# Three key units of a recurrent layer share each input tile, ahead of the low-rank projections

## The chip, the cores and the metric

The kernel runs on one core of one Trainium2 chip. The metric is the device time of one execution in microseconds (us), taken as the median of several runs.

## What is computed

One inference step of a two-layer decoder: layer A is a recurrent (delta-rule) layer, layer B an attention layer. Tokens stand in columns: 512 prompt columns and 32 sample columns, 544 in all; features are 1024 = 8 tiles of 128 partitions. Only the start of layer A matters here:

```
xn = rms_norm(x, ln_g)
prev = xn shifted by one token
mixed[i] = xn + mu[i] * (prev - xn)          # i = r, k, v, z, w, a
k = mixed[k] @ w_in[k]                       # 1024 x 1024: the key projection
w_low, a_low = tanh(mixed[w] @ w_la), mixed[a] @ a_la     # 64 columns each
kk = (k * k_k), divided per head by its norm
```

Everything that follows in layer A (decays, chunk products, state, group norm, gate, output projection) needs the keys and their norms, and layer B needs layer A.

## The kernel before

Work of the start, in the order of the program:

- The eight tiles of x are loaded and squared, and their sums give one factor per token. `norm` writes a tile of xn, `mix` (L302 to L311) makes a mixed tile: ScalarE scales xn (L305 for 512 columns, L306 for 32), VectorE adds the shifted part (L307, L309). `split` (L163) makes the exact pair of the mixed tile: the rounded part by ScalarE (L166) and the remainder by VectorE or GpSimd (L167), by the letters of `ENG["xk"] = "gvgvgggv"` (g is GpSimd, v is VectorE). These eight pairs are `xk`, kept until the last key unit.
- A unit is 128 output features: `load_w` (L126) brings 512 KB of weights into one of two `wst` buffers, ScalarE rounds them (L133, `whi`) and GpSimd subtracts (L134, `wlo`); each of `whi` and `wlo` has two buffers. `dense` (L143) then does three products per input tile, whi by x rounded, whi by x remainder, wlo by x rounded, for two column halves of 256 and 288: 48 matmuls a unit. A half has one PSUM bank of the two of pool `pd`. In some units (`BOTH`, among the key units 0, 4, 5, 6, 7) the two halves advance together over the input tiles, in the others one after the other.
- `kproj` (L351) is one key unit. Behind each half come a copy of the bank to SBUF on VectorE (L104), a square on ScalarE (L357) and a matmul with `sel` (L358) that adds the squares per head into `ssp`.
- `hidden` (H in the plan) does one input tile's part of the two low-rank projections: two mixes into the two buffers of pool `mp`, and matmuls into `hps`, both banks of pool `pu` (L378).

`PLAN` is a list of such steps by hand: H0 K0 K1 H1 ... is the order in which the program is written, with a number behind the letter. It is not quite the order on the engines. The context is opened with `schedule_with_timeline_sim=True`, and a scheduler with a timeline of its own picks, for each engine, among the steps that it takes to be ready; the plan's order is their priority. Each engine then runs its list in order.

PSUM has eight banks: two each in `pd` (projections), `pt` (`ssp` in this stage), `pu` (`hps` in this stage) and `pc` (unused in this stage). Pool `bp` (tag B, ten buffers of 128 x 1088) first serves the chunk operands of a later stage.

Of the kernel before, what the change touches and what calls it, by code (L numbers as in the profile page):

```python
# [6 lines left out]
F32 = mybir.dt.float32  # L7
F32R = mybir.dt.float32r
# [6 lines left out]
P = 128  # L15
D = 1024
KT = 8
# [41 lines left out]
NR = 2  # L59
PLAN = """H0 K0 K1 H1 H2 H3 H4 H5 K2 H6 H7 K3 K4 K5 K6 K7 X3 r0 r7 N a0 r1 a1 b0 e0 b1 e1 T0  # L60
X2 r2 r3 a3 r4 a2 r6 r5 X0 v1 v3 v0 b3 e3 M0 P0 F0 F1 F2 v2 C0 C1 b2 o1 F3 C2 C3 M1
# [17 lines left out]
class Kern:  # L79
# [45 lines left out]

    def load_w(self, src, gain=None):  # L126
        nc = self.nc
        st = self.wst.tile([P, KT, P], F32, name="wst", tag="wst")
        nc.sync.dma_start(out=st, in_=src)
        hi = self.whl.tile([P, KT, P], F32R, name="whi", tag="whi")  # L130
        lo = self.whl.tile([P, KT, P], F32R, name="wlo", tag="wlo")
        if gain is None:
            nc.scalar.copy(hi, st)  # L133
            nc.gpsimd.tensor_tensor(lo, st, hi.bitcast(F32), op=ALU.subtract)  # L134
        else:
            for kt in range(KT):
                g = self.prm[:, gain, kt:kt + 1]
                nc.scalar.mul(hi[:, kt], st[:, kt], g)  # L138
                nc.vector.scalar_tensor_tensor(lo[:, kt], st[:, kt], g, hi[:, kt].bitcast(F32),  # L139
                                               op0=ALU.mult, op1=ALU.subtract)  # L140
        return hi, lo

    def dense(self, w, xs, evac, both=False):  # L143
        """three exact-part passes; both: the two column halves advance together over the inner tiles"""
        nc = self.nc
# [8 lines left out]
        for hfs in (((0, 1),) if both else ((0,), (1,))):  # L154
# [4 lines left out]
            for hf in hfs:  # L159
                c0, n = HALF[hf]  # L160
                evac(hf, c0, n, ps[hf][:, :n])

    def split(self, src, name, eng=None):  # L163
        nc = self.nc
        hi, lo = self.xpair(name)
        nc.scalar.copy(hi, src)  # L166
        (eng or nc.vector).tensor_tensor(lo, src, hi.bitcast(F32), op=ALU.subtract)  # L167
        return hi, lo

    def sq_add(self, tot, x, kt, tmp, halves=False):  # L170
        """squares of the features, summed over the tiles"""
        for c0, n in HALF if halves else ((0, NT),):
# [7 lines left out]
    def rms(self, sq, psum, sp):  # L180
        """1 / rms per token in every partition (PSUM); sq: squares summed over the tiles"""
        nc = self.nc
# [16 lines left out]

# [1 line left out]
    def layer_a(self):  # L201
        tc, nc, I, O, prm = self.tc, self.nc, self.I, self.O, self.prm
        with ExitStack() as ctx:
# [49 lines left out]

# [1 line left out]
            xt = []  # L255
# [27 lines left out]

# [1 line left out]
            sq8 = H_("sq8")  # L285
# [39 lines left out]
            def inv_rows(d):  # L325
                """reciprocal of rows in DRAM, spread over the partitions"""
                n = d.shape[0] * d.shape[1] // P
# [13 lines left out]

# [1 line left out]
            xk = []  # L343
            for kt in range(KT):
                norm(kt)
# [4 lines left out]

            def kproj(p):  # L351
                t = H_("kT")

                def evac(hf, c0, n, ps):
# [4 lines left out]
                                     start=(p == 0), stop=(p == 7))  # L359
                self.dense(self.load_w(W[p]), xk, evac, both=p in BOTH)  # L360
                if p < NR:
                    kT[p] = t
                else:
                    nc.sync.dma_start(out=scr["k"][p], in_=t)

            hps, la = [], []

            def hidden(kt):
                """one input tile's part of the low-rank hidden layers"""
                if kt == 0:  # L370
# [22 lines left out]

# [1 line left out]
            AL, RH, BK, AK = ([None] * 8 for _ in range(4))  # L395
# [41 lines left out]
            def pre_b(p):  # L437
# [7 lines left out]
                nc.vector.scalar_tensor_tensor(nb, ta, 1.0, kn, op0=ALU.add, op1=ALU.mult)  # L445
                # sample columns: alpha, rho, beta, kappa
                sq = sp.tile([P, 4, NS], F32, name="sq", tag="sq")
# [14 lines left out]
                self.eng("bk", p).tensor_tensor(bk[:, :, 64:128], c64(kp), ipv[:, :, 1:65], op=ALU.mult)  # L462
                # bonus sums
                nc.vector.scalar_tensor_tensor(kp, rT[p], pv(P_RK, p), kp, op0=ALU.mult, op1=ALU.mult)
# [4 lines left out]
            def pre_e(p):  # L469
                """bonus sums; the sample columns' products with the state"""  # L470
                kp, sq, st = POST[p]
# [4 lines left out]
                nc.sync.dma_start(out=scr["b"][p], in_=kp)  # L476
                # sample: token-major copies, products with the state
                ps = T8("sps")
# [50 lines left out]
            def tinv(g):  # L529
                """blocks of T = (1 - A)^-1 on the diagonal, for the chunks of two pairs: substitution,  # L530
                one lane per block and parity of the column; kept transposed"""
                a = tp.tile([P, 1024], F32, name="tA", tag="T", bufs=1)
# [21 lines left out]
            def tmerge(p):  # L554
                """the block below the diagonal: T21^T = T11^T (A21^T T22^T)"""
                g = p // 2
# [38 lines left out]
            def prechain(p):  # L595
                ak, bk, rh, t = AK[p], BK[p], RH[p], TT[p]
                w = ak.rearrange("p c h x -> p (c h x)")
                # stacked [T alpha; T A_kappa]
                WW[p] = w.rearrange("p (e c h x) -> p e c h x", e=2, c=4, h=2)
# [15 lines left out]
            def feed(p, i):  # L615
                """operands of two chunks: stacked [A_beta; A_kappa], keys against the end of the chunk, values"""
                bk, rh = BK[p], RH[p]
# [28 lines left out]
            def step(p, c2):  # L646
                """state in, [M0; V] or [V; M0] by head; its updates U, stacked [U; V]; state out; outputs"""
                uv = sp.tile([P, 2, 2, 64], F32, name="uv", tag="uv", bufs=2)
# [35 lines left out]
            def bonus(p):  # L684
                """bonus term and the norm's bias, kept in DRAM until the norm"""
                t = zp.tile([P, NT], F32, name="bsum", tag="Z")
# [54 lines left out]
            def gn_sample():  # L741
                """group norm, bonus of the sample columns of all pairs"""
                for p in range(8):
# [22 lines left out]
            def gn(g):  # L766
                """group norm of the prompt columns of two pairs: deviations, their reciprocals"""
                ssg, sqs = U8("ssg"), []
# [17 lines left out]
            def gn_apply(g):  # L786
                """norm, bonus"""
                normed.add(g)
# [8 lines left out]
            def zproj(p):  # L797
                """gate; applied at once where the norm comes first"""
                hold = p // 2 not in normed
# [44 lines left out]
            def xzsplit():  # L844
                for kt in range(KT):
# [3 lines left out]
            xv, xz = [], []  # L849
            fns = dict(K=kproj, H=hidden, N=lambda p: key_norms(), r=rproj, a=pre_a, b=pre_b, e=pre_e, T=tinv, v=vproj,  # L850
                       M=tmerge, P=prechain, F=lambda j: feed(j // 4, j % 4), C=lambda j: step(j // 4, j % 4), o=bonus,
# [5 lines left out]

# [1 line left out]
            gx = [self.split(Y[p], "g") for p in range(8)]  # L859
# [25 lines left out]

# [1 line left out]
    def layer_b(self):  # L887
        tc, nc, I, O, prm = self.tc, self.nc, self.I, self.O, self.prm
        with ExitStack() as ctx:
# [29 lines left out]

            # normalised input  # L920
            def load_h(kt):
# [70 lines left out]
            def scores(st, l):  # L992
                """scores and exponentials of the window (l = 0) or of the strided groups (l = 1)"""
                Q, K = st["Q"], st["K"]
# [32 lines left out]
            def join(st, p):  # L1027
                """factors that put both row orders on a common maximum and sum"""
                stats = [st["stats", l] for l in range(2)]
# [28 lines left out]
            def attend(st, i):  # L1058
                """weights transposed, times the values: window (own block, block before), two strided groups"""
                l, half, g = ((0, 1, 0), (0, 0, 0), (1, 0, 1), (1, 1, 2))[i]  # L1060
# [170 lines left out]

            # output projection, residual, final norm
            gx = [self.split(G[p], "g") for p in range(8)]
# [37 lines left out]
    def new_state(self):  # L1271
        """The recurrent state of the sample group after its tokens, on GpSimd."""
        tc, nc, I, O = self.tc, self.nc, self.I, self.O
# [38 lines left out]
def prep(inp):  # L1312
# [27 lines left out]
    c0, c1, c2 = (f[f"cache_kv_g{g}"].reshape(8, -1, 2, 4, 4, 64) for g in range(3))  # L1340
    # keys: [quad, b half, head pair, chunk, (head, c), b, 256 rows]; values: [quad, b half, chunk, 128 rows, b, (head, c)]
    rows = np.arange(128)
# [111 lines left out]
```

## Time and profile before

| what | us |
|---|---|
| median of 3 runs | 1532.63 |
| lowest, highest run | 1529.68, 1542.64 |
| span of the profiled execution | 1545.5 |
| TensorE busy in it | 1429.4 (92%) |

The profiled execution is one of its own; its span, from the first to the last instruction, is the only time that the profile gives for it. A line of the timeline has start, duration, engine, line of the kernel, operation, what is written from what, the shape, the count of instructions merged, and in brackets the idle time before it and what ended that. Matmuls overlap in time, so their step is read from their starts. The granted clock of a window is the profile's; what level TensorE had is read from the pace of the matmuls as well.

### The profile page before, as it was taken

The numbers are of one execution on the slowest core, as the hardware profiler recorded it, in microseconds if no ns is written. First come the engines' busy times: TensorE is split into PE (matmuls) and PEld (weight loads), VectorE is DVE, ScalarE is ACT, GpSimd is POOL, SyncE is SP. The second block draws the span as 40 slices with busy tenths as digits, with TensorE's granted clock in tenths as the row PEclk, the third lists the DMA queues.
The fourth block names the chain that finished last, engine by engine and source line by source line (L and its number), as shares of the span: only waits on it lengthen the run. The fifth ranks groups of instructions, "written<-read, shape, count | busy, mean of one in ns | idle before, by whom it ended". The sixth has DMA issues, their size and how long they took to land.

```text
span 1545.5 us, 32046 instructions
## 1 busy us (share of the span) xinstructions
PE 1429.4 (92%) x12144; PEld 1184.9 (77%) x12144; DVE 999.4 (65%) x2612; ACT 656.0 (42%) x1808; POOL 531.3 (34%) x763
## 2 busy tenths in 40 slices
PE   2998978998988989999989999999999999999996
PEld 2676966676767757998877788977889788897776
DVE  7429494748577356789995787745468455684635
ACT  5447452343433355344633335444345443554322
POOL 6125355434545122896776772000000000000111
PEclk9999978776869698999999999999999999999998
DMA  4123635233323024564345653445534366344543
GB/s 141 49 84 127 197 98 144 69 81 91 91 79 88 19 59 120 162 193 146 117 136 164 202 190 116 141 134 193 190 113 138 127 202 198 105 143 131 192 136 105
DMA packets 140586, 201.24 MB, mean 130 GB/s; under 512 B 76864, under 2 KB 80640, under 8 KB 140432
## 3 DMA queue, kind: packets, MB, share of 16 engines
q1 hardware_dynamic: 121456, 137.48, 29.7%
q10 hardware_dynamic: 16416, 54.41, 11.1%
q0 software_dynamic: 2560, 7.31, 1.4%
q8 instruction: 95, 1.56, 0.4%
q14 instruction: 59, 0.48, 0.1%
HBM read 150.90 MB, written 34.87 MB: 120 GB/s over the span
## 4 chain that ended last, share of the span: by engine, by line
PE 67%; DVE 17%; DMA 8%; ACT 3%; issue 2%; SPq 2%; POOL 0%; DVEq 0%; ACTq 0%; POOLq 0%
PE dps L152 39%; DVE wlo L139 3%; PE ops L1078 3%; PE sps L1015 2%; PE ptp L1070 2%; DVE tX L548 2%; PE sps L1011 2%; PE spo L1161 2%; PE sc L1117 1%; PE ops L1082 1%; DVE tT L546 1%; PE cps L675 1%; DMA ot<-exp 1%; PE cps L678 1%; PE hps L378 1%
## 5 line engine op out<-in xcount | busy, mean ns | idle before, releaser
L152 PE MATMUL dps<-hn,whi 128*128 128x256 f32 (+1 forms) x2560 | 512.0, 295 | 5.9 <-DVE ho L873 2.4
L152 PEld LDWEIGHTS dps<-hn,whi 128*128 128x128 f32 x2560 | 406.5, 190 | 30.3 <-issue 18.9
L152 PE MATMUL dps<-hn,wlo 128*128 128x288 f32 (+1 forms) x1280 | 377.5, 295 | 4.5 <-DVE wlo L139 4.3
L138 ACT ACTIVATE whi<-wst,prm 128x128 fp32r<-128x128 f32 x640 | 201.3, 391 | 224.5 <-PE dps L152 175.4
L139 DVE SCALAR_TENSOR_TENSOR wlo<-wst,prm,whi 128x128 fp32r<-128x128 f32 x640 | 251.9, 447 | 36.6 <-ACT whi L138 36.4
L152 PEld LDWEIGHTS dps<-hn,wlo 128*128 128x128 f32 x1280 | 243.1, 190 | 17.3 <-issue 8.8
L152 PE MATMUL dps<-x,whi 128*128 128x256 f32 (+1 forms) x1024 | 229.9, 317 | 27.2 <-ACT x L166 11.3
L152 PEld LDWEIGHTS dps<-x,whi 128*128 128x128 f32 x1024 | 178.4, 207 | 51.9 <-issue 16.2
L134 POOL TENSOR_TENSOR wlo<-wst,whi 128x1024 fp32r<-128x1024 f32 x48 | 118.6, 2472 | 201.2 <-ACT whi L133 186.2
L152 PE MATMUL dps<-x,wlo 128*128 128x288 f32 (+1 forms) x512 | 158.3, 310 | 0.0
L152 PEld LDWEIGHTS dps<-x,wlo 128*128 128x128 f32 x512 | 106.1, 207 | 2.7 <-issue 1.8
L1091 POOL COPY qd<-Q 64x32 f32<-64x32 f32 x48 | 16.5, 344 | 261.9 <-DVE Q L955 130.9
L152 PE MATMUL dps<-g,whi 128*128 128x288 f32 (+1 forms) x512 | 101.0, 294 | 1.8 <-DVE ho L869 1.2
L1289 POOL TENSOR_TENSOR sS<-sS,sT 128x256 f32<-128x256 f32 x128 | 98.9, 773 | 8.3
L1024 ACT ACTIVATE s<-s,nm 128x256 f32<-128x256 f32 (+1 forms) x128 | 61.8, 484 | 73.8 <-PE sc L1117 31.4
L133 ACT CAST whi<-wst 128x1024 fp32r<-128x1024 f32 x48 | 50.3, 1047 | 93.9 <-PE dps L152 55.2
L152 PEld LDWEIGHTS dps<-g,whi 128*128 128x128 f32 x512 | 81.4, 190 | 6.1 <-DVE g L167 2.4
L1098 POOL COPY pk<-vt 128x32 f32<-128x32 f32 x24 | 7.2, 298 | 205.9 <-DVE vt L964 125.2
L152 PE MATMUL dps<-g,wlo 128*128 128x256 f32 (+1 forms) x256 | 73.8, 289 | 0.0
L307 DVE SCALAR_TENSOR_TENSOR mix<-xn,prm,mix 128x512 f32<-128x512 f32 x48 | 42.4, 885 | 26.9 <-ACT mix L305 26.8
L671 DVE SCALAR_TENSOR_TENSOR mv<-mv,plp,cps 64x64 f32<-64x64 f32 x112 | 31.1, 278 | 43.3 <-PE cps L661 32.0
L104 ACT COPY uv<-cps 64x64 f32<-64x64 f32 x128 | 26.4, 207 | 75.0 <-PE cps L656 66.5
(317 smaller groups left out, 2557.4 us busy)
## 6 DMA issues: line engine op xcount, KB each, us to landing
wst<-in_wb SPq DMA_DIRECT2D x88, 512.0 KB
kc<-in_kc ACTq DMA_DIRECT2D x48, 512.0 KB
vc<-in_vc ACTq DMA_DIRECT2D x48, 512.0 KB
wst<-in_wa SPq DMA_DIRECT2D x40, 512.0 KB
swp<-nat SPq DMA_DIRECT2D x192, 68.0 KB
out_kT<-K SPq DMA_DIRECT2D x24, 272.0 KB
out_vT<-vt SPq DMA_DIRECT2D x24, 272.0 KB
xt<-in_xT SPq DMA_DIRECT2D x8, 272.0 KB
```

The lines of the kernel that those rows point to most:

```text
L133: nc.scalar.copy(hi, st)
L134: nc.gpsimd.tensor_tensor(lo, st, hi.bitcast(F32), op=ALU.subtract)
L138: nc.scalar.mul(hi[:, kt], st[:, kt], g)
L139: nc.vector.scalar_tensor_tensor(lo[:, kt], st[:, kt], g, hi[:, kt].bitcast(F32), op0=ALU.mult, op1=ALU.subtract)
L152: nc.tensor.matmul(ps[:, :n], lhsT=a[:, kt, :], rhs=x[:, c0:c0 + n], start=(kt == 0 and i == 0), stop=(kt == KT - 1 and i == 2))
L307: nc.vector.scalar_tensor_tensor(m[:, 0:NP_], xn[kt][:, 0:NP_], pv(s, kt), m[:, 0:NP_], op0=ALU.mult, op1=ALU.add)
L548: nc.vector.tensor_tensor(x3[:, s + 1:32, 0:w], x3[:, s + 1:32, 0:w], t, op=ALU.add)
L671: nc.vector.scalar_tensor_tensor(d[h], mv[r, e, h, :], plp[r, p, c:c + 1], ps[r, o + 64:o + 128], op0=ALU.mult, op1=ALU.add)
L1011: nc.tensor.matmul(ps[:, j, lo:], lhsT=Q[0][r, q], rhs=K[0][r, (b - 1) * P + lo:(b + 1) * P], start=True, stop=True)
L1024: nc.scalar.activation(s[:, b, lo:], s[:, b, lo:], AF.Exp, bias=nm[:, b:b + 1], accum_out=stats[:, b, h, 1:2])
L1078: nc.tensor.matmul(ov[r, :, 32 * b:32 * b + 32], lhsT=v[:, b - b0, r], rhs=pts[h][:, b].rearrange("p (i r) -> p r i", r=4), start=(half == ...
L1289: nc.gpsimd.tensor_tensor(s, s, t, op=ALU.add)
```

## The change

The plan begins with `L3 H0 H1 H2 H3 K3 H4 H5 H6 H7 K4 ...` in place of `H0 K0 K1 H1 H2 H3 H4 H5 K2 H6 H7 K3 K4 ...`. `L3` runs key units 0, 1 and 2 as one step: for each of the eight input tiles all three units' products for both halves, 18 matmuls a tile, in six banks (two each of `pd`, `pu` and `pc`). Only then come the six evacuations, the copy, square and `ssp` matmul as before, unit after unit. The three weight loads and their roundings are written ahead of the norm and the mixes; the third pair of `whi` and `wlo` takes two of the ten buffers of tag B, because the usual two pairs are held by units 0 and 1.

```diff
-PLAN = """H0 K0 K1 H1 H2 H3 H4 H5 K2 H6 H7 K3 K4 K5 K6 K7 X3 r0 r7 N a0 r1 a1 b0 e0 b1 e1 T0
+PLAN = """L3 H0 H1 H2 H3 K3 H4 H5 H6 H7 K4 K5 K6 K7 X3 r0 r7 N a0 r1 a1 b0 e0 b1 e1 T0
...
-    def load_w(self, src, gain=None):
+    def load_w(self, src, gain=None, spare=None):
...
-        hi = self.whl.tile([P, KT, P], F32R, name="whi", tag="whi")
-        lo = self.whl.tile([P, KT, P], F32R, name="wlo", tag="wlo")
+        if spare is None:
+            hi = self.whl.tile([P, KT, P], F32R, name="whi", tag="whi")
+            lo = self.whl.tile([P, KT, P], F32R, name="wlo", tag="wlo")
+        else:
+            hi, lo = (spare(n)[:, 0:KT * P].rearrange("p (a b) -> p a b", a=KT) for n in ("whs", "wls"))
...
+    def dense_together(self, ws, xs, pss, evacs):
+        nc = self.nc
+        for kt in range(KT):
+            xh, xl = xs[kt]
+            for (hi, lo), ps in zip(ws, pss):
+                for hf, (c0, n) in enumerate(HALF):
+                    for i, (a, x) in enumerate(((hi, xh), (hi, xl), (lo, xh))):
+                        nc.tensor.matmul(ps[hf][:, :n], lhsT=a[:, kt, :], rhs=x[:, c0:c0 + n],
+                                         start=(kt == 0 and i == 0), stop=(kt == KT - 1 and i == 2))
+        for ps, evac in zip(pss, evacs):
+            for hf, (c0, n) in enumerate(HALF):
+                evac(hf, c0, n, ps[hf][:, :n])
...
+            def spare_w(name):
+                return bp.tile([P, 2 * NT], F32R, name=name, tag="B")
+            lead_w = [self.load_w(W[p], spare=spare_w if p == 2 else None) for p in range(3)]
             for kt in range(KT):
                 norm(kt)
                 xk.append(self.split(mix(MU_K, kt, M_ if kt < 2 else H_), "x", self.eng("xk", kt)))
...
+            def kproj(p):
+                self.dense(self.load_w(W[p]), xk, kevac(p), both=p in BOTH)
+
+            def klead(n):
+                self.dense_together(lead_w, xk, [[pool.tile([P, 512], F32, name="dps", tag=tag) for _ in range(2)]
+                                                 for pool, tag in ((self.pd, "d"), (pu, "u"), (pc, "c"))],
+                                    [kevac(p) for p in range(n)])
```

`kevac` is the old evacuation of `kproj`, taken out as a function. The rest of the diff removes comments.

## Rows read from the trace of the kernel before

**Rows 1.** Page: busy time of the engines; granted clock in 40 slices.
```profile
PE 1429.4 (92%) x12144; PEld 1184.9 (77%) x12144; DVE 999.4 (65%) x2612; ACT 656.0 (42%) x1808; POOL 531.3 (34%) x763
...
PEclk9999978776869698999999999999999999999998
```

**Rows 2.** Windows: busy us and instructions per engine, granted clock, DMA share, GB/s.
```profile
20.00:30.00 10.00, 2.13 (x8) 1.81 (x8) 10.00 (x16) 9.65 (x21) 5.62 (x11) 1.00 0.31 105
30.00:40.00 10.00, 4.54 (x20) 4.22 (x20) 9.85 (x13) 3.00 (x6) 7.67 (x4) 1.00 0.00 0
...
50.00:60.00 10.00, 10.00 (x57) 6.73 (x57) 4.13 (x9) 4.49 (x9) 2.16 (x1) 1.00 0.17 53
...
100.00:110.00 10.00, 10.00 (x71) 8.21 (x70) 1.34 (x3) 3.37 (x5) 3.49 (x2) 1.00 0.31 108
...
260.00:400.00 140.00, 130.17 (x1487) 96.04 (x1486) 91.32 (x278) 50.81 (x140) 59.77 (x108) 0.71 0.32 84
```

**Rows 3.** Timeline, first matmuls of key unit 0 on TensorE.
```profile
28.69 0.58 PE L152 MATMUL dps<-x,whi 128*128 128x256 f32 x1 [1.14 <-POOL x L167]
...
35.89 0.58 PE L152 MATMUL dps<-x,whi 128*128 128x256 f32 x1 [5.46 <-DVE x L167]
```

**Rows 4.** Timeline, VectorE: mixes and splits.
```profile
25.02 0.25 DVE L309 SCALAR_TENSOR_TENSOR mix<-xn,prm,mix 128x32 f32<-128x32 f32 x1
...
29.28 1.36 DVE L309 SCALAR_TENSOR_TENSOR mix<-xn,prm,mix 128x32 f32<-128x32 f32 x1
...
35.12 1.35 DVE L167 TENSOR_TENSOR x<-mix,x 128x544 fp32r<-128x544 f32 x2
...
38.31 0.71 DVE L167 TENSOR_TENSOR x<-mix,x 128x544 fp32r<-128x544 f32 x1
```

**Rows 5.** Timeline, GpSimd: splits, and a later unit's weights.
```profile
26.77 10.90 POOL L167 TENSOR_TENSOR x<-mix,x 128x544 fp32r<-128x544 f32 x5 [0.77 <-ACT x L166]
47.09 2.38 POOL L134 TENSOR_TENSOR wlo<-wst,whi 128x1024 fp32r<-128x1024 f32 x1 [9.42 <-ACT whi L133]
```

**Rows 6.** Timeline, ScalarE: mixes, roundings, third unit's weights, a square.
```profile
19.87 0.72 ACT L305 ACTIVATE mix<-xn,omu 128x512 f32<-128x512 f32 x1 [1.87 <-DVE xn L297]
...
26.06 2.27 ACT L166 CAST x<-mix 128x544 fp32r<-128x544 f32 x4
...
45.96 1.05 ACT L133 CAST whi<-wst 128x1024 fp32r<-128x1024 f32 x1 [0.89 <-PE dps L152]
46.92 0.47 ACT L357 ACTIVATE sqk<-dps,prm 128x256 f32<-128x256 f32 x1
```

**Rows 7.** Chain of waits in order of time: start, us, what.
```profile
35.89 5.53 PE dps L152 x23
41.42 1.06 PE hps L378 x4
...
44.11 1.83 PE dps L152 x13
...
93.33 3.01 PE dps L152 x24
96.34 0.59 PE ssp L358 x2
96.93 3.38 PE dps L152 x24
...
111.98 3.26 PE dps L152 x23
...
119.01 0.42 ACT rs L390
...
126.20 1.55 DMA rows<-rinv
...
128.40 3.14 DMA rowb<-rows
```

**Rows 8.** Timeline, SyncE's queue: weight loads.
```profile
16.55 2.63 SPq L129 DMA_DIRECT2D wst<-in_wa x2
```

**Rows 9.** Windows of 2 us, columns as in rows 2: landings of those loads.
```profile
18.00:20.00 2.00, 1.04 (x5) 0.75 (x4) 1.96 (x7) 0.13 (x2) 1.95 (x10) 1.00 0.75 240
20.00:22.00 2.00, 0.00 (x0) 0.00 (x0) 2.00 (x4) 2.00 (x5) 0.58 (x4) 1.00 0.64 240
22.00:24.00 2.00, 0.00 (x0) 0.00 (x0) 2.00 (x4) 2.00 (x7) 0.57 (x4) 1.00 0.00 0
```

More of the change, by code (lines that the diff above doesn't have):

```diff
@@ L349, in layer_a, with kevac @@
             kT, rT, vT = [None] * 8, [None] * 8, [None] * 8
-            def kproj(p):
+            def kevac(p):
                 t = H_("kT")
@@ L359, in evac @@
                                      start=(p == 0), stop=(p == 7))
[L360 to L364, printed above, removed]
+                    if hf:
+                        if p < NR:
+                            kT[p] = t
+                        else:
+                            nc.sync.dma_start(out=scr["k"][p], in_=t)
+                return evac
+            def kproj(p):
[4 more added lines that the diff above has]
+                                    [kevac(p) for p in range(n)])
             hps, la = [], []
@@ L849, in layer_a @@
             xv, xz = [], []
-            fns = dict(K=kproj, H=hidden, N=lambda p: key_norms(), r=rproj, a=pre_a, b=pre_b, e=pre_e, T=tinv, v=vproj,
+            fns = dict(L=klead, K=kproj, H=hidden, N=lambda p: key_norms(), r=rproj, a=pre_a, b=pre_b, e=pre_e, T=tinv, v=vproj,
                        M=tmerge, P=prechain, F=lambda j: feed(j // 4, j % 4), C=lambda j: step(j // 4, j % 4), o=bonus,
```

## The prediction

> **What bounds the kernel now.** Read the page first: TensorE is busy 92% of the span, and its granted clock is full in the first slices and dips only in the slices of layer A's later stages [rows 1]. A new matmul order can therefore gain only where TensorE stands still or runs at its half level. The windows of 10 us show where that is at the start: between 20 and 40 us TensorE is busy 6.7 of 20 us while VectorE is full, and in the stage behind, at 50 and at 100 us, TensorE is busy 10 of 10 [rows 2]. The timeline names the stop: unit 0 begins its first tile at 28.69 us, and its next full step waits 5.46 us, until 35.89, for a split on VectorE [rows 3]. VectorE's own rows say why. The splits of tiles 1 and 3, which VectorE makes, come together at 35.12, behind the mixes; and while GpSimd runs its five splits without a break, 26.77 to 37.67 [rows 5], a 32-column mix takes 1.36 us that takes 0.25 otherwise [rows 4]. Tile 7's split ends last, at 39.0 [rows 4]. In the chain of waits, 23 matmuls then take 5.53 us, 0.240 each, and two later halves of 24 take 3.01 and 3.38 us, 0.133 each [rows 7]: unit 0 runs at about half the pace, the 1.2 GHz level (the windows print 1.00 there, so here the pace decides), and the 2.4 GHz level follows from about 41.4 us. From 35.89 to the end of unit 7 TensorE never waits; behind it come the key norms, two transfers of their rows and the decays, all in the chain [rows 7]. The stage is bound first by the mixing of the tiles, then by TensorE, and what it saves is handed on about one for one.
>
> **What the change adds before the matmuls.** No arithmetic is added. Of the three weight loads two stood at the front already. The third, one of two that SyncE issues at 16.55 us and behind it [rows 8], has landed by about 20 to 22 us, since no bytes move from 22 to 24 [rows 9]. What is new is that its rounding (1.05 us [rows 6]) and its subtraction (2.38 us [rows 5]) no longer wait for a buffer until 45.96 but enter ScalarE's and GpSimd's queues here. Queued behind the rounding are ScalarE's mixes, which begin at 19.87, and the roundings of the tiles, 26.06 on [rows 6]; ScalarE runs through from one to the other, so I count the whole 1.05 us on the tiles. GpSimd has little between 20 and 26 us (5.62 us busy in 20 to 30, of which 3.23 are the splits from 26.77 [rows 2, 5]); if the subtraction falls there it costs nothing, and if it lands ahead of the first split it costs up to 2.38. I take nothing, as the weights land well before 26 us; the upper end is a rival's.
>
> **What it moves in the tile loop.** Before, unit 0 has done 8 matmuls when it stops [rows 2], the six of tile 0 and two of tile 1 that need only the rounded part. With three units it is 18 and 6, so 24. The 16 extra ones take 16 x 0.240 = 3.8 us and fit into the stop of 5.46 us. I assume that VectorE keeps its order, since the queue of GpSimd that goes with it is unchanged; the restart is then at 35.89 + 1.05 = 36.94. The count of unit 0 to 2's 144 matmuls, without the other work of TensorE, which stays the same: before, 8 and 23 are done at 41.42, and the other 113 take 113 x 0.133 = 15.0, to 56.4 us. After, if the clock rises at 41.4 as before, 4.5 us at 0.240 give 18 more, 42 in all, and 102 x 0.133 = 13.6 lead to 54.9: 1.5 us gained. If the longer work ahead of the stop (24 matmuls, 5.8 us, against 8) raises the clock by 36.94 already, 120 x 0.133 = 16.0 lead to 52.9: 3.5 gained. No row shows this clock case; both ends stay, and I take 2.5, the middle.
>
> **The handover.** All six banks close within the last tile, and this adds a wait: unit 3's weights need the buffers of unit 0, free only at its last matmul, 12 matmuls (1.6 us) before the end of the step. Rounding and subtraction, 1.05 + 2.38 = 3.43 us, end 1.8 us after it. Queued meanwhile on ScalarE are six squares of 0.47 [rows 6], and behind each an `ssp` matmul pair of some 0.57 us on TensorE, 3.4 in all; H0's two groups of 1.06 [rows 7] wait for the `pu` banks, hence for the third and fourth squares. These 5.5 us cover 1.8 us if the squares come in time; the first can't before a copy and its own 0.47, and the rounding of 1.05 shares ScalarE with them. Bounds: nothing, if the cover is whole, to 3.4 us, if it is gone. I take 1.0, nearer to the cover. Then H0 to H3 follow with their mixes in two buffers, and unit 3's 48 matmuls fill between them, as units 1 and 2 do now. The banks of `pc` and the two buffers of tag B are unused in this stage; they cost nothing here, and whoever first needs them comes after 130 us.
>
> **Sum.** 2.5 - 1.0 = 1.5 us gained, between 1.9 lost (1.5 - 3.4) and 3.5 gained. The sum is made against the profiled execution, whose span of 1545.5 is 12.9 us above the median of the runs; a difference of this size in one stage carries over as it is: 1532.6 - 1.5 = 1531.1, between 1529.1 and 1534.5.
>
> **Does cycling over banks cost pace?** Unit 0 alternates over two banks in the traced kernel and 13 of its matmuls take 1.83 us once the clock is full, 0.141 each with the step into them, against 0.133 in units that stay in one bank [rows 7]: next to nothing. The Trainium skill, "TensorE: Matmul & The Clock Gate", section "A second HAM failure mode: psum-queue depth-cycling", speaks against this change: it tells of a kernel that cycled through banks, in which the engine idled briefly between groups and its clock went back and forth between the two levels. By that rule six banks would be worse than two; the trace, with two, does not agree, and six it does not show.
>
> **The rivals.** (1) *The tiles are taken at their pace.* The scheduler puts tile 1's split early, and TensorE runs through from about 29.7. At 0.240 for 5.53 us (what it took before the clock rose [rows 7]) it does 23 and, with six rounded-part products before, stands at 29 of 144 at 35.2; 115 x 0.133 = 15.3 lead to 50.5. Tile 7 at 40.1 doesn't bind. Gain 5.9 - 1.0 = 4.9: 1527.7. For it: the split waits on nothing but order, as its rounded part ends by 28.3 [rows 6]. Against: that order is the scheduler's, and nothing in the diff addresses VectorE. (2) *The third unit's weights come first, slower.* GpSimd runs the subtraction just ahead of tile 0's split; all five splits and VectorE's mixes beside them move by 1.05 + 2.38, and the restart is at 39.3. With 5.53 us at the half level, 47 are done at 44.8, and 97 x 0.133 lead to 57.7: 1.3 lost, and with an uncovered handover of 3.4 it is 4.7: 1537.3. It decides from a restart later than 38.0, where nothing is gained any more (38.0 + 5.5 + 12.9 = 56.4). For it: the load is written ahead of every mix. Against: the landing by 22 us. (3) *Bank cycling holds the clock at half*: 120 x 0.240 = 28.8 from 36.94 end at 65.7, 9.3 later, and 1.0 for the handover: 1542.9. (4) *The rest is reordered.* The scheduler's timeline is shifted, and it may pick another order far behind. From 260 to 400 us the granted clock is 0.71 [rows 2], that is, it changes between the levels there; 0.05 more or less would be 140 x 0.05 / 0.71 = 9.9 us, so about 1522 or 1542, either way. For it: this stretch is the most broken one. Against: the plan from X3 on is the same. (5) *The change does its part and nothing is handed on*, because ScalarE's mixes for the next unit end later: 1532.6. Against: the chain goes through TensorE to the last key unit.
>
> **How the numbers follow.** Forecast 0.40; (1) 0.15; (2) 0.15; (3) 0.03; (4) 0.20, half each way; (5) 0.07. The predicted time is 1531.1. The range, 1521 to 1541, takes in the forecast's bounds, (1), (2), (5) and the faster side of (4), and leaves out the slower side and (3), 0.13, and some of the tails. A measurement of this kernel tells about 1% (15.3 us) from no change: the runs shown lie 13 us apart. All first-stage cases are inside that. Only (4) at one and a half times its price passes it, and (3) nearly: 0.07 faster, 0.86 within, 0.07 slower.
>
> **What would show it.** Right: matmuls of three units between 28 and 34 us, a stop until about 37 for a split on VectorE, the last of the 144 at about 53 to 55 us, less than 1 us of TensorE idle behind it, and the last `ssp` one to three us earlier. If VectorE makes tile 1's split before 31 us, (1) holds; if GpSimd's L134 for the third unit ends after 26 us, (2); if matmuls of the step still lie 0.240 apart after 45 us, (3). If the start moves as told and the time doesn't, compare the stages behind 120 us by span and clock: (4) or (5). The prediction is wrong in its base if matmuls of the low-rank layers or of unit 3 leave TensorE open for several us, or if the later stages move by more than the first.

## The result and the profile after

| kernel | runs | median us | lowest, highest |
|---|---|---|---|
| before | 20 | 1538.51 | 1525.61, 1551.55 |
| changed | 20 | 1550.32 | 1538.49, 1560.78 |

The ratio is 1.0069, with an interval of 1.0045 to 1.0093: the change makes the kernel slower by 0.7%, some 10.6 us. The median of before over 20 runs lies 6 us above that of the three runs shown ahead, and single executions of one kernel lie over 20 us apart. So a profile, which is one execution, may say less than the runs: the profiled execution of the changed kernel has a span of 1539.1 us, near its fastest, and that of before, 1545.5, is among its slower ones.

The page of the changed kernel, busy time and granted clock in 40 slices, answers to [rows 1]:

```profile
PE 1423.4 (92%) x12144; PEld 1182.4 (77%) x12144; DVE 1002.3 (65%) x2612; ACT 654.2 (43%) x1808; POOL 528.8 (34%) x763
...
PEclk9998959967867699999999999999999999999998
```

Nothing stands out there. The start does what the change is made for. The timeline of TensorE, answering to [rows 3]:

```profile
27.39 1.27 PE L174 MATMUL dps<-x,whi 128*128 128x256 f32 x4 [8.85 <-ACT x L183]
28.46 0.66 PE L174 MATMUL dps<-x,whs 128*128 128x256 f32 x2
...
31.23 0.37 PE L174 MATMUL dps<-x,wls 128*128 128x256 f32 x1
31.43 0.30 PE L174 MATMUL dps<-x,whs 128*128 128x288 f32 x1
31.57 0.30 PE L174 MATMUL dps<-x,wls 128*128 128x288 f32 x1
...
32.21 0.41 PE L174 MATMUL dps<-x,whs 128*128 128x256 f32 x2
34.31 0.39 PE L174 MATMUL dps<-x,whi 128*128 128x256 f32 x1 [1.70 <-DVE x L184]
```

The stop of 5.46 us is down to 1.70 us. VectorE, ScalarE and GpSimd show why (timelines, answering to [rows 4 to 6]). The first line is VectorE's first step of `norm` before the change, the second the same step after it:

```profile
17.08 1.36 DVE L297 SCALAR_TENSOR_TENSOR xn<-xt,prm,rsum 128x32 f32<-128x32 f32 x8 [0.72 <-PE rsum L196]
```

```profile
16.57 1.36 DVE L314 SCALAR_TENSOR_TENSOR xn<-xt,prm,rsum 128x32 f32<-128x32 f32 x8 [0.72 <-PE rsum L213]
...
26.82 0.24 DVE L326 SCALAR_TENSOR_TENSOR mix<-xn,prm,mix 128x32 f32<-128x32 f32 x1
...
27.65 1.38 DVE L326 SCALAR_TENSOR_TENSOR mix<-xn,prm,mix 128x32 f32<-128x32 f32 x1
...
33.55 1.35 DVE L184 TENSOR_TENSOR x<-mix,x 128x544 fp32r<-128x544 f32 x2
...
19.57 1.04 ACT L136 CAST whs<-wst 128x1024 fp32r<-128x1024 f32 x1 [2.08 <-DMA wst<-in_wa]
...
20.70 2.36 POOL L137 TENSOR_TENSOR wls<-wst,whs 128x1024 fp32r<-128x1024 f32 x1 [1.12 <-ACT whs L136]
...
27.42 10.45 POOL L184 TENSOR_TENSOR x<-mix,x 128x544 fp32r<-128x544 f32 x5 [1.92 <-ACT x L183]
```

The third unit's weights come at 19.57 and 20.70 us. Nothing waits for GpSimd there; ScalarE's mixes begin behind the rounding, at 20.52 us. The profiled execution of the changed kernel is 0.51 us ahead of that of before when `norm` begins, at 16.57 against 17.08 us. This differs between executions (16.25 to 18.12 us in the traces of all runs) and is no part of the change, so it has to be taken off. The five splits of GpSimd begin 0.65 us later than before, which is 1.16 us later counted from `norm`, about the third unit's rounding. VectorE gets one more mix done at 0.24 us ahead of them: up to the splits of tiles 1 and 3 three mixes are held up beside them, not four. So these splits start at 33.55 us, 1.57 us earlier, of which 0.51 is the earlier execution and 1.06 the mix. In the traces of the runs further down they begin 18.02 to 18.04 us after `norm` in every one with the old start and 16.96 to 16.98 in every one with the new. The chain of waits, answering to [rows 7]:

```profile
34.31 15.24 PE dps L174 x120
49.56 0.54 PE ssp L379 x2
50.09 0.43 PE dps L155 x2
50.53 0.59 PE ssp L379 x2
```

120 matmuls in 15.24 us are 0.127 each: the clock is at its 2.4 GHz level from the end of the stop on. It was there ahead of the stop too: the starts, 0.20 us or more apart up to 31.43 us, are 0.13 to 0.14 apart from there on, and the 1.70 us of the stop don't bring the old pace back. The step ends at 49.6 us and there is no gap behind it; `ssp` and unit 3 take turns. The last `ssp`, timeline of TensorE, before and after:

```profile
117.75 0.66 PE L358 MATMUL ssp<-sqk,sel 128*16 128x288 f32 x2
```

```profile
111.51 0.61 PE L379 MATMUL ssp<-sqk,sel 128*16 128x256 f32 x2 [2.09 <-ACT sqk L378]
...
113.08 0.66 PE L379 MATMUL ssp<-sqk,sel 128*16 128x288 f32 x2
```

It ends at 113.7 us, before at 118.4. So this profile is 4.7 us ahead by then, 4.2 without the earlier `norm`, although TensorE has a new wait of 2.09 us at 111.5 us, for a square that ScalarE makes behind mixes for r and another unit's weights. With 10.6 us lost in all, about 15 us are lost behind.

### The profile page after: what moved, and what is told of

Read it like the earlier page. It is cut to its first block, busy times and chain, and to the rows that moved or that the text cites. A ratio compares the mean times of both kernels' runs of the same rounds, so it can differ in the third digit from the quotient of the medians.

```text
span 1539.1 us, 32035 instructions
## 1 busy us (share of the span) xinstructions
PE 1423.4 (92%) x12144; PEld 1182.4 (77%) x12144; DVE 1002.3 (65%) x2612; ACT 654.2 (43%) x1808; POOL 528.8 (34%) x763
## 3 DMA queue, kind: packets, MB, share of 16 engines
q10 hardware_dynamic: 16416, 54.41, 10.6%
## 4 chain that ended last, share of the span: by engine, by line
PE 64%; DVE 19%; DMA 8%; ACT 4%; issue 3%; SPq 2%; POOL 0%; ACTq 0%; DVEq 0%; POOLq 0%
PE dps L155 37%; DVE wlo L142 3%; PE ops L1109 3%; PE sps L1046 2%; DVE tX L579 2%; PE ptp L1101 2%; PE sps L1042 2%; DVE tT L577 2%; PE spo L1192 2%; PE sc L1148 1%; PE ops L1113 1%; DMA ot<-exp 1%; PE hps L409 1%; PE dps L174 1%; PE cps L709 1%
## 5 line engine op out<-in xcount | busy, mean ns | idle before, releaser
L155 PE MATMUL dps<-x,whi 128*128 128x288 f32 (+1 forms) x928 | 212.4, 321 | 13.1 <-DVE zth L838 2.9
L155 PEld LDWEIGHTS dps<-x,whi 128*128 128x128 f32 x928 | 163.5, 209 | 35.2 <-issue 13.1
L137 POOL TENSOR_TENSOR wlo<-wst,whi 128x1024 fp32r<-128x1024 f32 x47 | 114.6, 2439 | 207.2 <-ACT whi L136 145.8
L155 PE MATMUL dps<-x,wlo 128*128 128x256 f32 (+1 forms) x464 | 144.0, 312 | 0.0
L155 PEld LDWEIGHTS dps<-x,wlo 128*128 128x128 f32 x464 | 97.5, 211 | 5.1 <-issue 4.8
```

Source lines behind the costliest of these rows:

```text
L155: nc.tensor.matmul(ps[:, :n], lhsT=a[:, kt, :], rhs=x[:, c0:c0 + n], start=(kt == 0 and i == 0), stop=(kt == KT - 1 and i == 2))
```

## The experiments

**Two starts, two orders.** Behind unit 7 the program of both kernels is the same, instruction for instruction: the lists of the five engines hold 5497 from the mixes for r to the end of layer A. Their order on the engines is not. The scheduler's lists for TensorE, VectorE, ScalarE, GpSimd and SyncE all differ there; in layer B none does. So each engine's list can be written out and given to the other kernel, as edges that set the order of issue and add no wait of their own:

```diff
+def replay(nc, tc, start):
+    seen = [i for i in nc.cur_bb.bb.instructions][start:]
+    info = mybir.DependencyInfo(mybir.DependencyClass.NoSync, mybir.DependencyReason.DATA)
+    for part in zlib.decompress(base64.b85decode(ORDER)).decode().split(";"):
+        at, last = 0, None
+        for d in part.split(":")[1].split(","):
+            at += int(d)
+            if last is not None:
+                tc.add_manual_dep(seen[at], last.name, info, reason="replay")
+            last = seen[at]
...
             for tok in PLAN.split():
+                if tok == "X3":
+                    self.tail = len(nc.cur_bb.bb.instructions)
```

`new_again` is the changed kernel with its own lists, which gives the same program as the changed kernel:

> The changed kernel once more; its issue order behind the key units is written out, instruction by instruction, but is the one it had, so it is the same program. Theory A (the start gains some 4.7 us by the last ssp matmul, and the order that the scheduler gives to the rest of layer A loses some 15 us on average): ratio to before 1.005 to 1.009, last ssp near 113.7 us. Theory B (the earlier single profile with 1539.1 us is the rule, the loss is drift between chips): ratio 0.996 to 1.002.

`new_head_old_rest` is the changed kernel with the lists of before, `old_head_new_rest` the kernel before with the lists of the changed one:

> The changed start (three units together, new plan up to unit 7), but from the mixes for r on every engine issues layer A in the order of the kernel before. Theory A (the reordered rest is the loss): faster than before by the start's gain, 1532.6 to 1534.5 where before has 1538.5, ratio 0.996 to 0.999. Theory B (the start itself, its clock or its wait at the handover, costs later): slower as the change was, ratio 1.005 to 1.009. Theory C (a gain at the start is always lost again at the transfers of the key norms): ratio 1.000.

> The start of the kernel before, and from the mixes for r on the issue order that the changed kernel has. Theory A: slower by the loss without the gain, about 15 us, ratio 1.008 to 1.012. Theory B: as before, ratio 0.999 to 1.001. Theory C: like A without the part of the gain, ratio 1.005 to 1.009.

`plan_only_old_rest` is the kernel before, its own lists behind the start, and this edit:

```diff
-PLAN = """H0 K0 K1 H1 H2 H3 H4 H5 K2 H6 H7 K3 K4 K5 K6 K7 X3
+PLAN = """K0 K1 K2 H0 H1 H2 H3 K3 H4 H5 H6 H7 K4 K5 K6 K7 X3
```

> The kernel before with only the plan of the start changed (units 0, 1, 2 one after the other, then the low-rank projections as in the change; no shared tiles), the rest issued in the order of the kernel before. If sharing the tiles is what gains at the start: the stop of some 5.5 us before about 35.9 us is back, last ssp at 117 to 120 us, ratio 0.999 to 1.002. If moving the low-rank projections behind is what gains: last ssp near 113.7, ratio 0.996 to 0.999.

| label | start | order behind | ratio | interval | mean clock, before beside it |
|---|---|---|---|---|---|
| new_again | new | new | 1.0102 | 1.0063 to 1.0141 | 0.916, 0.930 |
| new_head_old_rest | new | old | 0.9984 | 0.9955 to 1.0013 | 0.927, 0.930 |
| old_head_new_rest | old | new | 1.0098 | 1.0060 to 1.0135 | 0.922, 0.930 |
| plan_only_old_rest | plan only | old | 0.9993 | 0.9958 to 1.0029 | 0.928, 0.930 |

The time goes with the order behind the start, not with the start, as theory A says; theory B falls with the second and third row. `new_again`, at 1.0102, lost more than the 1.009 that was expected, and its last `ssp` ends at 114.9 us. Theory C is not settled by the ratios: the second row's interval takes in its 1.000, the third row's its 1.005 to 1.009. In `plan_only_old_rest` the stop is back (5.45 us), and the last `ssp` ends at 123.9 us, beyond the 117 to 120 expected; `norm` begins 1.04 us later there than in the profile of before. So the plan alone gains nothing at the start; the sharing of the tiles does.

Whether the gain of the start is carried on can be read less clearly. The last `ssp` of `new_head_old_rest`, timeline of TensorE:

```profile
113.62 1.03 PE L431 MATMUL ssp<-sqk,sel 128*16 128x256 f32 x2 [3.95 <-ACT sqk L430]
...
116.16 1.14 PE L431 MATMUL ssp<-sqk,sel 128*16 128x288 f32 x2
```

It ends at 117.3 us, 1.1 ahead of before, and in the second run of this kernel, further down, 0.1 ahead. With the old lists TensorE waits 3.95 us for a square, not 2.09, and then runs at about half its pace for some us. Counted from `norm`, 0.9 of the 4.2 us are left at the last `ssp` in both. So this kernel holds the old order at the price of most of the start's gain. The last low-rank matmuls of layer A, timeline of TensorE, first before and then `new_head_old_rest`:

```profile
394.90 0.81 PE L411 MATMUL lps<-hid,lb 64*128 64x288 f32 x4
```

```profile
391.47 0.81 PE L494 MATMUL lps<-hid,lb 64*128 64x288 f32 x4
```

It is 3.4 us ahead there, but the distance is not that of the start: the first of these matmuls, near 117 us, is 0.5 us behind before, and matmul for matmul the profile is 0.8 to 3.4 us ahead between 170 and 420 us. `plan_only_old_rest` is 3.3 us behind at the same place, after 5.5 at the last `ssp`. So these profiles don't show that the gain is carried on.

**What the new order costs.** Two things can be read. The first is the clock. In the 27 runs of before that the ratios of these four go by, the time follows the mean granted clock of the run by about 11 us for 0.01 (1528.0 us at 0.938, 1549.3 at 0.923), with times up to 7 us apart at one clock (0.927). The new order has the lower clock: 0.922 against 0.930 in `old_head_new_rest`, by this slope about 9 of its 15 us in the mean, and 0.916 in `new_again`, some 15.5 of its 18.4. That is an estimate: the runs show that clock and time go together, not which of the two brings the other. With 11 us for 0.01 taken out, `old_head_new_rest` is still 6.5 us slower than before, and `new_head_old_rest` 4.5 us faster. The second is TensorE's open time. Windows of 260 to 420 us (busy us and instructions per engine, granted clock, DMA), in turn before, the changed kernel, `new_again`, `old_head_new_rest`:

```profile
260.00:420.00 160.00, 149.22 (x1701) 111.35 (x1700) 104.06 (x314) 58.80 (x163) 72.80 (x132) 0.71 0.31 80
```

```profile
260.00:420.00 160.00, 141.23 (x1790) 109.06 (x1789) 108.49 (x331) 62.04 (x174) 70.76 (x130) 0.79 0.37 92
```

```profile
260.00:420.00 160.00, 142.88 (x1551) 106.95 (x1551) 103.72 (x316) 54.70 (x152) 62.14 (x117) 0.66 0.31 79
```

```profile
260.00:420.00 160.00, 142.18 (x1869) 109.18 (x1867) 111.01 (x337) 61.98 (x170) 73.70 (x134) 0.80 0.36 89
```

With the old order TensorE is busy 149 of 160 us, with the new one 141 to 143. But the window does not hold the same work in each (1551 to 1869 matmuls). The second and third row are the same program: 0.79 and 0.66 of the clock, and 1539.1 and 1562.2 us of span. The clock differs from one execution to the next by more than the two orders do, so its part is read from the runs, not from one profile.

The same work, 4676 to 4679 matmuls, lies between the end of the last `ssp` and the first matmul of layer A's output projection (`dps<-g`). Worked out from the traces, with two runs that follow below:

| profile | order behind | stretch, us | TensorE open in it, us | granted clock |
|---|---|---|---|---|
| before | old | 498.8 | 54.9 | 0.79 |
| new_head_old_rest | old | 490.8 | 50.4 | 0.80 |
| new_head_old_vector | old for VectorE | 494.2 | 50.4 | 0.80 |
| changed | new | 498.5 | 56.5 | 0.79 |
| new_again | new | 515.5 | 60.4 | 0.76 |
| old_head_new_rest | new | 500.6 | 59.7 | 0.80 |
| old_head_new_first70 | new for VectorE's first 70 | 501.8 | 53.6 | 0.78 |

Behind the stretch all seven take 927 to 932 us to their end, so the loss lies in the stretch. It is some 9.5 us longer with the new order in the mean; TensorE is open for some 5.6 of these, though not in every pair of profiles, and busy for the rest.

**Which engine, which step.** The next four give VectorE's list alone, whole or in part, and leave all else to the scheduler.

```diff
-ORDER = <lists of all five engines>
+ORDER = <VectorE's list>                      # new_head_old_vector
+ORDER = <VectorE's list, entries 195 to 344>  # new_head_old_T1, old_head_new_T1
+ORDER = <VectorE's list, entries 345 to 489>  # new_head_old_T2
```

T1 and T2 are substitutions on VectorE for pairs 2, 3 and 4, 5. In the new order T1 begins behind F0 to F2, not ahead of them, and T2 ahead of several steps that it followed.

> The changed start; behind it only VectorE's issue order is that of the kernel before, the other engines are left to the scheduler. Theory V (VectorE's order leads, the other engines follow it): ratio 0.996 to 1.000, as with all five orders. Theory E (the loss is in the orders of the other engines): 1.005 to 1.010.

> The changed start; behind it only 150 instructions of VectorE are put in the order of the kernel before, those around step T1 (the substitution for pairs 2 and 3): 17 of T1's instructions ahead of F0, where the changed kernel issues F0 to F2 and the first of C0 ahead of T1. Theory T1 (this late start of T1 is the loss): ratio 0.996 to 1.001, T1 done some 16 us earlier than in the changed kernel. Theory T2 (the loss comes from the later swap, T2 ahead of a6, b6, F12 to F14, C12 and C7): 1.005 to 1.010.

> The changed start; behind it only the 145 next instructions of VectorE are in the order of the kernel before, those around step T2; T1 stays late, as in the changed kernel. Theory T1: 1.005 to 1.012. Theory T2: 0.996 to 1.001.

> The start of the kernel before; behind it only the 150 instructions of VectorE around T1 are in the order of the changed kernel, T1 late. Theory T1: slower by the loss alone, 1.008 to 1.012. Theory T2: 0.999 to 1.002.

| label | ratio | interval |
|---|---|---|
| new_head_old_vector | 1.0001 | 0.9982 to 1.0021 |
| new_head_old_T1 | 1.0167 | 1.0138 to 1.0196 |
| new_head_old_T2 | 1.0085 | 1.0055 to 1.0114 |
| old_head_new_T1 | 1.0041 | 1.0019 to 1.0063 |

VectorE's order is enough: with it alone the loss is gone, and the other engines come out nearly as before (in the traces TensorE's instructions are 1.5 places off those of before in the mean, against 9.7 for the changed kernel). The theory of T1 falls: with T1 back in its old place the kernel is slower still, 1.0167. The theory of T2 falls with the next row. The last row, 1.0041, fits neither theory. A piece of one order set into the other is not half of the loss.

**Where the orders part.** VectorE's first 40 instructions behind the start, worked out from the two programs; a letter is a step of the plan (X3 mixes for r, N key norms, X2 mixes for z, a0 and b0 the first decays and keys), with its count:

```
before   g6 X3x8 N X3x3 N X3x8 N X3x4 X2x2 a0 X2x2 a0x4 b0x2 X2x2
changed  g6 X3x11 N X3x5 N X3x5 N X3x2 X2x4 a0 X2x4 a0x2 b0x2
```

In the changed kernel four more of VectorE's instructions for z pass ahead of the last two of a0, and the key norms come some places later.

```diff
-ORDER = <VectorE's list>
+ORDER = <VectorE's list, first 40 entries>   # new_head_old_first40
+ORDER = <VectorE's list, first 70 entries>   # old_head_new_first70
```

> The changed start; behind it only VectorE's first 40 instructions (mixes for r, key norms, the first decays and mixes for z) are in the order of the kernel before, all else is left to the scheduler. Theory fork (the two orders part at once, where mixes for z pass the first decays, and the loss hangs on that): ratio 0.996 to 1.002. Rival (the loss comes from later turns that the scheduler takes for itself, whatever the first 40 do): 1.005 to 1.010.

> The start of the kernel before; behind it only VectorE's first 70 instructions are in the order of the changed kernel. Theory fork: 1.006 to 1.012, slower by the loss alone. Rival: 0.999 to 1.002.

`three_then_K3` is the changed kernel, all left to the scheduler, with another plan:

```diff
-PLAN = """L3 H0 H1 H2 H3 K3 H4 H5 H6 H7 K4 K5 K6 K7 X3
+PLAN = """L3 K3 H0 H1 H2 H3 H4 H5 K4 H6 H7 K5 K6 K7 X3
```

> The changed kernel with another plan behind the three units: L3 K3 H0 H1 H2 H3 H4 H5 K4 H6 H7 K5 K6 K7, order left to the scheduler. The order behind the start is then a third one, between the two. If the order of the rest decides, its time may lie anywhere from 0.995 to 1.015; if only the start counted it would be 0.997 to 0.999.

And `new_head_old_rest` a second time:

> Once more the changed start with all of the old order behind it, for a narrower interval. If the gain of the start is carried to the end: 0.996 to 0.999; if nothing is carried: 1.000.

| label | ratio | interval |
|---|---|---|
| new_head_old_first40 | 1.0019 | 0.9981 to 1.0057 |
| old_head_new_first70 | 1.0096 | 1.0060 to 1.0131 |
| three_then_K3 | 1.0148 | 1.0104 to 1.0192 |
| new_head_old_rest_2 | 0.9991 | 0.9953 to 1.0028 |

40 instructions of VectorE, put back, take the loss away as far as the interval tells (it reaches up to 1.0057), and 70 of the new order bring all of it to the old start. The scheduler's timeline parts there and takes all later turns from it: forty instructions held, and VectorE's instructions come out 1.1 places from those of before in the traces, not 9.6. A third plan gives a third order and 1.5%. With the order of before, the changed start gives 0.9984 and 0.9991, with VectorE's list alone 1.0001, with its first 40 entries 1.0019; all four intervals take in 1, so a gain of the start is not shown in the time, and no version here is shown faster than before. The profile of `new_head_old_first40` is the one that keeps the start: its last `ssp` ends at 113.9 us, 4.5 ahead of before, and at the low-rank matmuls near 140 us, behind the two transfers of the key norms, 4.2 are still there. So theory C, a loss at these transfers, does not hold in that execution.

## Why the prediction was wrong

**The step that failed** is the end of the sum: "a difference of this size in one stage carries over as it is". It carries over only if the order behind stays, and the scheduler wrote a new one. Rival (4) named this, with 0.20 and both signs, and priced it at 9.9 us by the clock of 260 to 400 us; against it stood "the plan from X3 on is the same". That was no reason: the plan only ranks the steps, and which one is ready first comes from a timeline that the change moves by a few us. Measured, the new order costs about 15 us on the old start (15.4 in the mean of the runs, 1.0098), and the changed kernel lost 10.6 in all. The prediction's own sign for this, later stages that move by more than the first, came. That this is near the rival's 9.9 is luck: its price was a lower clock from 260 to 400 us, and the profile of the changed kernel has 0.77 there, not less than 0.71.

**The base** of the sum was a median of three runs, 1532.63 us; over 20 runs it is 1538.51. Of the 19.2 us between 1531.1 and 1550.32, this is 5.9. The other 13.3 are the 11.8 by which the two medians differ and the 1.5 forecast.

**The restart** was taken as 35.89 + 1.05 = 36.94 us. The third unit's rounding did shift the tiles' roundings, by 1.16 us counted from `norm`, as the term said. But the later start of GpSimd's splits let VectorE pass one more mix, and the restart came at 34.31, 1.58 us earlier than before and not 1.05 later; 0.51 of that is the earlier execution. A delay on one engine of a pair that hold each other up can be a gain on the other (here a mix of 0.24 us in place of 1.36); counting the rounding on VectorE's splits had the wrong sign.

**The clock at the restart** was left between two ends, and the upper one is what came: 0.127 us per matmul after the restart. It had risen at 31.4 us, within the 24 matmuls ahead of the stop, and this is the reason that the upper end gave: the longer work there.

**The handover** was taken as 1.0 us, with 0 to 3.4 as bounds. It is the lower end: unit 3's first matmuls run between the `ssp` pairs from 50.09 us, and TensorE has no gap. The cover that the term weighed was whole.

**The gain at the start** was 2.5 before the handover and 1.5 after; 4.7 was measured by the last `ssp`, 4.2 without the earlier `norm`. That this is near rival (1)'s 4.9 is luck, since TensorE still stops once, and the new wait of 2.09 us at unit 7 is in neither sum. With all the old lists behind, 1.1 and 0.1 of the 4.7 are left at the last `ssp`.

**Rival (2)** didn't come: the subtraction ended at 23.1 us, as the landing of the weights said. **Rival (3)** didn't either. Six banks in turn ran at 0.127 us a matmul, against 0.133 in one bank. The Trainium skill ("TensorE: Matmul & The Clock Gate", "A second HAM failure mode: psum-queue depth-cycling") tells of a clock that goes back and forth where TensorE idles briefly between groups; behind the stop these traces show neither, with two banks or with six, and the 120 matmuls follow one another without a gap. **Rival (5)**, nothing handed on, can't be told from a small gain: held to the old order the changed start gives 0.9984 to 1.0019.

**What stays open**: why the new order goes with a lower clock (0.922 and 0.916 against 0.930) and leaves TensorE open some 6 us longer in the rest of layer A. No single step was found that does it; T1 and T2 were tried and neither explains it.

## What to carry to other kernels

Where a scheduler with a timeline of its own orders the engines, an edit early in the program is two edits: its own, and a new order for all that follows. Compare the order behind the edit first, and where it differs, hold it (edges of issue order from the old list) to see what the edit itself is worth; hold no more of it than is needed, since the whole old list cost the start here most of its gain. An early gain of some us can't be weighed against a reordering of one per cent by one profile of each kernel.

## What was not expected of the hardware

One program's executions differ by 1.5% (1528.0 to 1550.6 us in 27 runs of before), and most of that goes with the granted clock, 0.939 to 0.923, about 11 us for 0.01. And a start of GpSimd's splits 1.16 us later, counted from `norm`, gave VectorE 1.06 us, by one 32-column mix that took 0.24 us and not 1.36.
